# A decoder layer on one core: gates of one branch by exponential and logarithm, mLSTM in chunks of 128 tokens, and a final norm partly centred by matmuls

## The chip, the core and the metric

The kernel runs on one core of a Trainium2 chip. The metric is the device time of one launch in microseconds, the median of repeated executions. The core has a matrix engine (TensorE, PE in the profile; its weight loads are listed as PEld), three engines for elementwise work (VectorE or DVE, ScalarE or ACT, GpSimd or POOL) and a queue for transfers (SyncE, SP). Each engine works through its own instruction list in order, and semaphores make one engine wait for another.

## The reference, cut to what matters

One decoder layer is applied to a prompt of 256 tokens and to 8 single-token samples (264 columns together), everything in float32. Four token mixers run on one projection of the input and are merged by sigmoid gates; then come memory attention and an MLP with squared ReLU, each closed by a layer norm.

```python
def token_mixers(x, st, p):
    proj = x @ p["w_in"] + p["b_in"]
    ...                                   # A delta rule, B conv width 31, C short conv, D mLSTM
    out_c = bg_c * u_c
    h, C_new, n_new, m_new = mlstm_chunked(q, k, v, i_d, log_sigmoid(f_d), C_d, n_d, m_d)
    branches = jnp.stack([out_a, out_b, out_c, out_d], axis=2)
    proj_br = jnp.einsum("btnw,nwd->btnd", branches, p["w_branch"])
    gates = jax.nn.sigmoid(gate_pre.reshape(bn, T, N_BRANCH, D_MODEL))
    y = jnp.sum(gates * proj_br, axis=2) @ p["w_out"]

def step(carry, inp):                     # mLSTM, one chunk of tokens; the result doesn't depend on its length
    m_tok = jnp.maximum(b_c + m[..., None], mi_c)
    inter = jnp.exp(b_c + m[..., None] - m_tok)
    dmat = jnp.exp(ld_c - m_tok[..., None]) * qk_c
    num = inter * (q_c @ C) + dmat @ v_c
    den = inter * (q_c @ n) + sum(dmat)
    h = num / max(|den|, exp(-m_tok))
    C = scale * C + (k_c * wgt).T @ v_c

x = layer_norm(DN_ALPHA * x + sq_relu_mlp(x, p), p["ln3_g"], p["ln3_b"])
```

## The kernel before, in words

All activations stand with 128 features on the partitions and the 264 tokens in the free dimension. A large product is a list of "slots": each slot is one 128 by 1024 tile of weights (512 KB), loaded by SP into `raw`, rounded by ACT into `wh` (line 123), and the remainder `wl` = `raw` - `wh` is formed by DVE or, every few slots, by POOL (line 128). TensorE then issues 24 matmuls per slot (`mm3`, all named `g` in the profile): high by high, low by high, high by low. `feed` and `feed_lo` work two slots ahead of the matmuls.

Between slots, `run` steps generators that hold the smaller work: `chain` holds the delta rule of branch A (`a_unit`, four units of two heads) and then the mLSTM of branch D (`d_unit`, two units of two heads). A scheduler of the framework fixes the final order of each engine's list when the program is built. PSUM has two pools of four banks: `g` for the slots, `b` for everything else, handed out in turn.

Three places matter here. (1) `phase2(2, "C", True)` makes the first 16 gates and projected blocks of the merge, those of the short convolution (branch C). Its gate is `act(..., AF.Sigmoid)` straight from PSUM. The last unit of branch A and the blocks b4 to b7 of branch B run between its slots; they use the helper `sigmoid` (lines 163 to 171 hold it and `rsqrt_small`), which takes a minimum on DVE and then exponential, logarithm and exponential on ACT. `ACT_TABLE_LOAD` is the instruction that brings the tables of another function set into ACT.

(2) `d_unit` walks over four chunks of 64 tokens (`CH`). Both heads of a chunk share one PSUM bank `nb`: head 0 on partitions 0 to 63, head 1 on 64 to 127. A chunk's matmuls are `nb` from the state `C` and the queries (not in the first chunk), `nb` from the weights within the chunk (`QK`, named `m_dt`) and the values `vt`, and `cb`, the update of the state, one per head. Then a few operations on 128x1 columns (`dn`) and two passes of ACT over `nb` into `hs`, transposes `hb`, and `c_upd`, which handles four sample tokens (its matmuls are `nr`). A float32 matmul leaves two records in the trace.

(3) `tail` ends the program. `Norm.finish(True)` makes mean and 1/deviation of the last layer norm from four float32 matmuls (`s`, `q`), then `TAIL` lists eleven groups of the 16 blocks: subtract the mean, multiply by 1/deviation, apply gain and offset, send. The first of the two numbers is the count of blocks, the second says whether POOL (1) or DVE (0) does the two passes; `FIN` names two blocks whose gain and offset are on DVE, the others are on ACT.

Of the kernel before, what the change touches and what calls it, by code (L numbers as in the profile page):

```python
# [17 lines left out]
P = 128  # L18
# [11 lines left out]
NCH = NP // CH  # L30
ALPHA = 2.0 ** 0.25
# [11 lines left out]
TAIL = ((1, 0), (2, 0), (1, 1), (2, 0), (1, 1), (2, 0), (1, 1), (2, 0), (1, 1), (2, 0), (1, 0))  # L43
FIN = (11, 14)
# [40 lines left out]
for _name, _w in (("ident", 128), ("eye", 64), ("incl", 64), ("m1u", 64), ("m1t", 64), ("reset", 256)):  # L85
    _cc[_name] = (_n, _w)
    _n += _w
# [4 lines left out]
def decoder_step(ctx, tc, A, O):  # L92
# [55 lines left out]
    def mm(out, lhsT, rhs, start=True, stop=True):  # L148
        PE.matmul(out, lhsT, rhs, start=start, stop=stop)  # L149
# [234 lines left out]
    class Norm:  # L384
# [19 lines left out]
        def finish(self, last=False):  # L404
# [3 lines left out]
            for j, b in ((0, bs), (1, bq)):  # L408
                x = [a[i][:, j] if j or self.first[i] is True else self.first[i] for i in range(2)]
                if not last:  # L410
                    tt(a[0][:, j], a[0][:, j], x.pop(), ADD)
                for i, y in enumerate(x):
                    mm(b, ones, y, start=i == 0, stop=i == len(x) - 1)
            d, q = a[1][:, 0], a[1][:, 1]
            act(a[0][:, 0], bs, AF.Square, scale=n)
            act(d, bs, AF.Copy, scale=n)
# [20 lines left out]
    RD = w1.tile([P, 2, CH], F32R, name="RD")  # L437
# [6 lines left out]
    c3 = w1.tile([P, NCH, 2], F32, name="c3")  # L444
# [4 lines left out]
    GP.tensor_copy(RD[:].rearrange("p f l -> p (f l)"), zero[:].to_broadcast([P, 2 * CH]))  # L449
# [27 lines left out]
    m0, na, mp = sml[:, 0:NS], sml[:, 8:9], sml[:, 16:16 + NCH]  # L477
# [7 lines left out]
    def row_stage():  # L485
# [74 lines left out]
        cpy(d0[rD, CH:NP:CH], rb[rD, CH - 1:NP - 1:CH])  # L560
# [14 lines left out]
        for i, src in enumerate((lD, rD, lD, rD)):  # L575
            rv = RR[src, 0, 0:NP].rearrange("p (f c l) -> p f c l", f=2, c=2)
            act(RD[32 * i:32 * i + 4], rv[:, :, i // 2, :].bitcast(F32), AF.Copy)
        yield
        wg = e[rD, :]
        tt(ch(wg[:, 0:NP]), ch(LB), lastb(M, HD), SUB)  # L580
# [14 lines left out]
        for c in range(NCH):  # L595
            for hh in range(2):
                mm(b[64 * hh:64 * hh + 64, 2 * c:2 * c + 2], RR[:, 2, c * CH:(c + 1) * CH].bitcast(F32), selr[:, 8 + hh:12:2].bitcast(F32))
        cpy(c3[:].rearrange("p a b -> p (a b)"), b[:, :2 * NCH])
# [439 lines left out]
    def phase2(n, pair, first, between={}):  # L1038
        for d in range(KB):
# [3 lines left out]
            def post_g(ps, bc, d=d, st=st):  # L1043
# [3 lines left out]
                last["SIG"] = act(st["s"][:], ps, AF.Sigmoid, bias=bc)  # L1047
# [64 lines left out]
    def d_unit(u):  # L1112
# [3 lines left out]
        sh = [P, 2, 2, CH]  # L1116
        KQ = v4(bank("KQd"))
        G = bank("Gd")[:, :256].rearrange("p (h f l) -> p h f l", h=2, f=2)
# [37 lines left out]
        cpy(sl[:], ib[:, :, CH - 1:NP:CH])  # L1156
# [82 lines left out]
        for c in range(NCH):  # L1239
            hf, o = c // 2, slice(CH * (c % 2), CH * (c % 2) + CH)  # L1240
            t = slice(c * CH, c * CH + CH)
            nb = bank("nb")
            if c:
                for hh in range(2):
# [13 lines left out]
            dn = tp.tile([P, 3], F32, tag="dn", name="dn")  # L1258
            hs = w1.tile([P, 2, NP], F32, tag="wT", name="hs")
            dd, ss, rs = (dn[:, i:i + 1] for i in range(3))  # L1260
            ts(dd, nb[:, 256:257], -1.0, MUL, c3[:, c, u:u + 1], MAX)
            act(hs[:, 0], nb[:, 0:256], AF.Square, accum_out=ss)
            tt(dd, dd, nb[:, 256:257], MAX)
            recip(dd, dd)
            stt(ss, ss, dd, dd, MUL, MUL)
            rsqrt_small(rs, ss, 1.0 / 256, RMS_EPS)
            tt(rs, rs, dd, MUL)
            act(hs[:, 1], nb[:, 0:256], AF.Copy, scale=rs)
            yield
            yield from c_upd(c)  # L1270
            hb = bank("hb")[:, :256].rearrange("p (w h t) -> p w h t", w=2, h=2)
            for w in range(2):
                PE.transpose(hb[:, w].rearrange("p h t -> p (h t)"), hs[:, 1, w * P:(w + 1) * P], ident)
            for w in range(2):
                act(ho[:, :, w, t], hb[:, w], AF.Copy, scale=col("dnw", w))
# [637 lines left out]
```

## Time and profile before

| what | value |
|---|---|
| median of 3 runs | 2297.16 us (2295.27 to 2297.56) |
| the profiled execution's own time | 2294.18 us |
| its span in the trace | 2292.4 us |
| PE busy | 2239.1 us, 98% of the span |
| DVE, ACT, POOL busy | 1285.0, 1200.6, 932.1 us |
| matmul records | 19034 |

The span runs from the first to the last instruction of the program in the trace. "Busy" is the time in which an engine worked on at least one instruction; for PE it is the union of overlapping matmuls. The records of idle time name the engine whose instruction ended the wait.

### The profile page before, as it was taken

What the parts mean: (1) busy time and instruction counts of PE and PEld (TensorE: products, weight loads), DVE (VectorE), ACT (ScalarE), POOL (GpSimd) and SP (SyncE); (2) the same over time, 40 slices, a digit from 0 to 9 for tenths busy, and PEclk for the clock granted to TensorE, in tenths of its full rate; (3) what the DMA queues carried; (4) which work ended last, traced back from release to release, by engine and by line L of the source; (5) the groups of instructions that cost most, each with busy time, mean ns of one, the idle gap of its engine ahead of it and who ended that gap; (6) DMA issues with size and microseconds to landing.
All of it is one profiled execution on the core that took longest, in us unless ns stands there. A gap on an engine that the chain in (4) does not pass through costs nothing.

```text
span 2292.4 us, 46436 instructions
## 1 busy us (share of the span) xinstructions
PE 2239.1 (98%) x19034; PEld 2197.2 (96%) x19034; DVE 1285.0 (56%) x2054; ACT 1200.6 (52%) x1823; POOL 932.1 (41%) x703
## 2 busy tenths in 40 slices
PE   9899999998999999999999999999999999999997
PEld 9899999898999999999999999999999999999996
DVE  7978778576678555443465465587324324423433
ACT  6755545855566555444444454465435435534543
POOL 3523434322223123343223364136445444544576
PEclk9999999999999999999999999999999999999998
DMA  7545566454565576666566667555665566566653
GB/s 251 160 150 185 161 180 193 135 173 143 174 187 178 194 217 204 215 198 180 181 219 179 194 207 233 183 168 169 188 182 176 178 184 178 173 185 183 176 180 115
DMA packets 125134, 418.81 MB, mean 183 GB/s; under 512 B 15608, under 2 KB 20984, under 8 KB 124920
## 3 DMA queue, kind: packets, MB, share of 16 engines
q1 hardware_dynamic: 124920, 415.84, 59.1%
q8 instruction: 149, 2.44, 0.5%
q14 instruction: 65, 0.53, 0.1%
HBM read 401.37 MB, written 14.41 MB: 181 GB/s over the span
## 4 chain that ended last, share of the span: by engine, by line
PE 84%; DVE 8%; ACT 4%; issue 2%; POOL 1%; DMA 1%; SPq 0%; DVEq 0%; ACTq 0%; POOLq 0%
PE g L149 74%; PE q L149 3%; DVE wl L128 2%; ACT L123 1%; DVE cB L138 1%; DVE cu L138 1%; PE pv L149 1%; ACT wh L123 1%; DVE s L138 1%; DVE y L128 1%; DMA dbc<-dd 1%; PE xb L149 0%; PE ob L149 0%; PE ub L149 0%; ACT sg L123 0%
## 5 line engine op out<-in xcount | busy, mean ns | idle before, releaser
L123 ACT ACTIVATE wh<-raw 128x1024 fp32r<-128x1024 f32 (+1 forms) x705 | 744.0, 1057 | 766.7 <-PE g L149 594.3
L128 POOL TENSOR_TENSOR wl<-raw,wh 128x1024 fp32r<-128x1024 f32 x234 | 571.3, 2441 | 652.8 <-PE g L149 466.5
L149 PE MATMUL g<-xh,wl 128*128 128x264 f32 x2496 | 712.2, 285 | 6.7 <-DVE wl L128 6.6
L128 DVE TENSOR_TENSOR wl<-raw,wh 128x1024 fp32r<-128x1024 f32 (+1 forms) x471 | 591.5, 1256 | 226.2 <-PE g L149 129.2
L149 PE MATMUL g<-xh,wh 128*128 128x264 f32 x2496 | 717.1, 287 | 0.0
L149 PE MATMUL g<-xl,wh 128*128 128x264 f32 x2496 | 714.0, 286 | 0.0
L149 PEld LDWEIGHTS g<-xh,wl 128*128 128x128 f32 x2496 | 471.2, 189 | 9.4 <-DVE wl L128 8.0
L149 PEld LDWEIGHTS g<-xh,wh 128*128 128x128 f32 x2496 | 471.9, 189 | 5.8 <-issue 3.4
L149 PEld LDWEIGHTS g<-xl,wh 128*128 128x128 f32 x2496 | 470.5, 189 | 1.2 <-issue 0.8
L149 PE MATMUL g<-hgh,wl 128*128 128x264 f32 x1024 | 290.4, 284 | 0.0
L149 PE MATMUL g<-hgl,wh 128*128 128x264 f32 x1024 | 290.4, 284 | 0.0
L149 PE MATMUL g<-hgh,wh 128*128 128x264 f32 x1024 | 289.9, 284 | 0.0
L149 PE MATMUL g<-zh,wh 128*128 128x266 f32 x960 | 275.0, 286 | 0.0
L149 PE MATMUL g<-zh,wl 128*128 128x266 f32 x960 | 274.9, 286 | 0.1
L149 PE MATMUL g<-zl,wh 128*128 128x266 f32 x960 | 274.6, 286 | 0.0
L149 PEld LDWEIGHTS g<-hgl,wh 128*128 128x128 f32 x1024 | 193.0, 188 | 0.0
L149 PEld LDWEIGHTS g<-hgh,wh 128*128 128x128 f32 x1024 | 192.6, 188 | 0.0
L149 PEld LDWEIGHTS g<-hgh,wl 128*128 128x128 f32 x1024 | 192.3, 188 | 0.0
L149 PEld LDWEIGHTS g<-zl,wh 128*128 128x128 f32 x960 | 181.7, 189 | 0.0
L149 PEld LDWEIGHTS g<-zh,wl 128*128 128x128 f32 x960 | 180.8, 188 | 0.8 <-POOL wl L128 0.8
L149 PEld LDWEIGHTS g<-zh,wh 128*128 128x128 f32 x960 | 181.4, 189 | 0.0
L128 DVE TENSOR_TENSOR hgl<-relu,hgh 128x264 fp32r<-128x264 f32 x64 | 60.7, 950 | 173.7 <-ACT hgh L123 173.7
(482 smaller groups left out, 3436.8 us busy)
## 6 DMA issues: line engine op xcount, KB each, us to landing
raw<-in_win_dram SPq DMA_DIRECT2D x312, 512.0 KB, 4.0
raw<-in_f_dram SPq DMA_DIRECT2D x248, 512.0 KB, 4.0
raw<-in_wbr_dram SPq DMA_DIRECT2D x64, 512.0 KB, 4.3
raw<-in_wout_dram SPq DMA_DIRECT2D x32, 512.0 KB, 4.2
s<-in_sS_dram SPq DMA_DIRECT2D x8, 512.0 KB, 5.3
dbc<-dd SPq DMA_DIRECT2D x16, 256.0 KB, 4.1
out_S_s_dram<-s SPq DMA_DIRECT2D x8, 512.0 KB, 5.3
c<-in_sCm_dram SPq DMA_DIRECT2D x8, 512.0 KB, 5.4
```

Source lines behind the costliest of these rows:

```text
L123: return AC.activation(out, in_, func, bias=bias, scale=scale, **kw)
L128: return (eng or DV).tensor_tensor(out=out, in0=a, in1=b, op=op)
L138: return DV.scalar_tensor_tensor(out=out, in0=a, scalar=s, in1=b, op0=op0, op1=op1)
L149: PE.matmul(out, lhsT, rhs, start=start, stop=stop)
```

## The change

It has three parts.

First, `phase2` with `n == 2` calls `sigmoid(st["s"], ps, bc)`: a DVE operation that adds the bias and bounds from below, then Exp, Ln and Exp on ACT. The other three phases keep `AF.Sigmoid`.

Second, `d_unit` walks over two chunks of 128 tokens (`CD`). The decay matrix `E` and the weights `QK` are now 128 by 128 per head and chunk; `QK` lies in `UB`, a tile that branch A no longer needs then. Each head gets its own bank `nb` with all 128 partitions as tokens. `row_stage` makes the scans and columns for chunks of 128 (the 16 small matmul records of `emT` become four, and the four copies into `RD` go).

Third, in `tail` the negative mean is kept; blocks 10 to 15 are centred on PE (identity times block, plus identity times negative mean, both float32, into six PSUM banks), and DVE alone does the passes: "s" adds the negative mean to two blocks, "m" multiplies two blocks by 1/deviation, "p" multiplies one block from PSUM. All gains and offsets are on ACT; POOL does nothing in it.

```diff
-TAIL = ((1, 0), (2, 0), (1, 1), (2, 0), (1, 1), (2, 0), (1, 1), (2, 0), (1, 1), (2, 0), (1, 0))
-FIN = (11, 14)
+PE_TAIL = 10
+TAIL = (("s", 0, 2), ("s", 2, 2), ("m", 0, 2), ("p", 10, 1), ("s", 4, 2), ("m", 2, 2), ("p", 11, 1), ("m", 4, 2),
+        ("s", 6, 2), ("p", 12, 1), ("m", 6, 2), ("s", 8, 2), ("p", 13, 1), ("m", 8, 2), ("p", 14, 1), ("p", 15, 1))
...
-            act(d, bs, AF.Copy, scale=n)
+            act(d, bs, AF.Copy, scale=-n if last else n)
...
-                last["SIG"] = act(st["s"][:], ps, AF.Sigmoid, bias=bc)
+                if n == 2:
+                    sigmoid(st["s"][:], ps, bc)
+                else:
+                    last["SIG"] = act(st["s"][:], ps, AF.Sigmoid, bias=bc)
...
-            mm(G[:, hh], selc(h0 + hh), RD[:])
-        for hf, hh, o, t in each():
-            mm(KQ[o, hf, hh], k[:, hh, t], q[:, hh, t])
-        E, QK = mat("m_dl"), mat("m_dt")
+            mm(G[:, hh], sel(8 + h0 + hh, P), RR[:, 0, 0:NP])
+        for hf in range(2):
+            for hh in range(2):
+                t = slice(hf * P, hf * P + P)
+                mm(KQ[:, hf, hh], k[:, hh, t], q[:, hh, t])
+        QK = UB
...
-        for c in range(NCH):
-            hf, o = c // 2, slice(CH * (c % 2), CH * (c % 2) + CH)
-            t = slice(c * CH, c * CH + CH)
-            nb = bank("nb")
-            if c:
-                for hh in range(2):
-                    mm(nb[64 * hh:64 * hh + 64, :257], qi[:, hh, t], C[:, hh, :], stop=False)
+        for c in range(NCD):
+            t = slice(c * CD, c * CD + CD)
+            nbs = [bank("nb") for hh in range(2)]
             for hh in range(2):
-                mm(nb[64 * hh:64 * hh + 64, :257], QK[o, hf, hh], vt[o, hf, hh, :], start=c == 0)
+                if c:
+                    mm(nbs[hh][:, :257], qi[:, hh, t], C[:, hh, :], stop=False)
+                mm(nbs[hh][:, :257], QK[:, c, hh], vt[:, c, hh, :], start=c == 0)
...
-                mm(cbs[hh], kw[o, hf, hh], vt[o, hf, hh])
+                mm(cbs[hh], kw[:, c, hh], vt[:, c, hh])
...
+        for d in range(PE_TAIL, KB):
+            ps = (gbank if d < PE_TAIL + 4 else bank)("ctr")[:, :NT]
+            last["PE"] = after(mm(ps, ident, y3[:, d, :], start=True, stop=False), "PE")
+            mm(ps, ident, ln.mu, start=False, stop=True)
+            centred[d] = ps
+        def step_(i, n, kind):
+            t = y3[:, i:i + n, :]
+            if kind == "s":
+                x = tt(t, t, ln.mu[:, None, :].to_broadcast([P, n, NT]), ADD)
+            elif kind == "m":
+                x = tt(t, t, ln.rs[:, None, :].to_broadcast([P, n, NT]), MUL)
+            else:
+                x = tt(y3[:, i, :], centred[i], ln.rs, MUL)
+            last["T"] = after(x, "T")
+            if kind == "s":
+                return
+            for j in range(i, i + n):
+                act(y3[:, j, :], y3[:, j, :], AF.Identity, bias=col("l3b", j), scale=col("l3g", j))
+            SP.dma_start(O["y"][:, i:i + n, :], t)
```

How the order of instructions moves at three places. ACT while the last unit of branch A normalises its queries and keys (`rq`, `rk`) and a block of branch B makes its gate (`gB`), between the slots of `phase2(2)`; before:

```order
L123 ACT_TABLE_LOAD
L123 ACTIVATE gB<-gB 128x264
L123 ACT_TABLE_LOAD
L123 ACTIVATE rk<-ssk,eps 128x2x256
L123 ACT_TABLE_LOAD
L123 ACTIVATE rq<-rq 128x528
L123 ACT_TABLE_LOAD
L123 ACTIVATE gB<-gB,ones 128x264
L123 ACTIVATE wh<-raw 128x1024
L123 ACT_TABLE_LOAD
L123 ACTIVATE gB<-gB 128x264
L123 ACT_TABLE_LOAD
```

and now, with `gate` the gate of branch C:

```order
L127 ACTIVATE gB<-gB 128x264
L127 ACTIVATE rk<-ssk,eps 128x2x256
L127 ACTIVATE rq<-rq 128x528
L127 ACTIVATE gB<-gB,ones 128x264
L127 ACTIVATE wh<-raw 128x1024
L127 ACTIVATE gB<-gB 128x264
L127 ACTIVATE rk<-ss_6597,eps 128x2x8
L127 ACTIVATE rk<-rk 128x528
L127 ACTIVATE cB<-extB,pc 128x256
L127 ACTIVATE wh<-raw 128x1024
L127 ACTIVATE gate<-gate 128x264
L127 ACTIVATE gate<-gate,ones 128x264
```

The loads are gone, and each `gate` has three operations. In the whole list of ACT there are 50 loads before and 7 now.

TensorE at a chunk of the first mLSTM unit that has a state (`hs` the normalised output, `vtD` the values, `kwD` the weighted keys); before, one of three such chunks of 64 tokens:

```order
L149 MATMUL g<-xh,wl 128x264
L1273 MATMUL hb<-cst,hs 128x128 x2
L149 MATMUL nb<-C,qkvD 64x257 x2
L149 MATMUL nb<-vtD,m_dt 64x257 x2
L149 MATMUL cb<-vtD,kwD 128x257 x2
L149 MATMUL g<-xh,wh 128x264
```

and now, the only one, of 128 tokens:

```order
L153 MATMUL g<-xh,wl 128x264
L153 MATMUL nb<-C,qkvD 128x257
L153 MATMUL nb<-vtD,UB 128x257
L153 MATMUL nb<-C,qkvD 128x257
L153 MATMUL nb<-vtD,UB 128x257
L153 MATMUL cb<-vtD,kwD 128x257 x2
L153 MATMUL g<-xh,wh 128x264
```

The shapes are output partitions by columns: the two 64-partition halves of `nb` have become two full matmuls, and the chunk occurs once instead of three times. The first `nr` afterwards follows 24 `g` later in both.

The tail on DVE (`a` holds mean and 1/deviation, 128x528 is two blocks), before:

```order
L138 SCALAR_TENSOR_TENSOR a_26062<-q,a_26061 128x264
L128 TENSOR_TENSOR y<-y,a_26062 128x264
L128 TENSOR_TENSOR y<-y,a_26062 128x528
L128 TENSOR_TENSOR y<-y,a_26062 128x264
L128 TENSOR_TENSOR y<-y,a_26062 128x528 x8
L128 TENSOR_TENSOR y<-y,a_26062 128x264
L128 TENSOR_TENSOR y<-y,a_26062 128x528
L134 TENSOR_SCALAR y<-y,pc 128x264
L128 TENSOR_TENSOR y<-y,a_26062 128x264
L134 TENSOR_SCALAR y<-y,pc 128x264
```

and now:

```order
L142 SCALAR_TENSOR_TENSOR a_26028<-q,a_26027 128x264
L132 TENSOR_TENSOR y<-y,a_26028 128x528 x3
L132 TENSOR_TENSOR y<-ctr,a_26028 128x264
L132 TENSOR_TENSOR y<-y,a_26028 128x528 x2
L132 TENSOR_TENSOR y<-ctr,a_26028 128x264
L132 TENSOR_TENSOR y<-y,a_26028 128x528 x2
L132 TENSOR_TENSOR y<-ctr,a_26028 128x264
L132 TENSOR_TENSOR y<-y,a_26028 128x528 x2
L132 TENSOR_TENSOR y<-ctr,a_26028 128x264
L132 TENSOR_TENSOR y<-y,a_26028 128x528
L132 TENSOR_TENSOR y<-ctr,a_26028 128x264 x2
```

with TensorE's last rows now

```order
L153 MATMUL s<-a_26027,ones 128x264
L153 MATMUL q<-a_26027,ones 128x264
L153 MATMUL s<-y,ones 128x264
L153 MATMUL q<-a_26028,ones 128x264
L153 MATMUL ctr<-y,cst 128x264 x6
L153 MATMUL ctr<-a_26028,cst 128x264 x6
```

DVE has taken over what POOL did, and TensorE issues all six products with the blocks before the six with the mean.

## Rows read from the trace of the kernel before

**Rows 1.** The page of the profile: busy time, share and instructions of PE, and the clock granted to it in 40 slices of the span (9 is 90% or more of full speed).

```profile
PE 2239.1 (98%) x19034; PEld 2197.2 (96%) x19034; DVE 1285.0 (56%) x2054; ACT 1200.6 (52%) x1823; POOL 932.1 (41%) x703
...
PEclk9999999999999999999999999999999999999998
```

**Rows 2.** Busy time by stretch: limits and length of the stretch in us, then busy us (and instructions) of each engine, PE's granted clock, the share of the transfer engines and GB/s.

```profile
50.00:100.00 50.00, 44.16 (x352) 42.61 (x351) 46.12 (x82) 36.98 (x72) 32.30 (x40) 0.93 0.46 141
100.00:375.00 275.00, 269.97 (x2561) 262.90 (x2560) 215.09 (x381) 148.32 (x264) 109.37 (x129) 1.00 0.57 174
400.00:655.00 255.00, 234.43 (x2175) 228.35 (x2174) 168.33 (x301) 171.45 (x252) 74.30 (x80) 0.98 0.52 158
757.00:972.00 215.00, 215.00 (x1752) 200.44 (x1751) 110.39 (x227) 111.27 (x187) 65.17 (x43) 1.00 0.68 210
524.70:528.80 4.10, 4.08 (x26) 3.75 (x27) 3.52 (x9) 4.05 (x5) 0.93 (x2) 0.50 0.45 132
```

**Rows 3.** Waits of PE between 400 and 655 us: waiting operation, the instruction it waited for, us in total, times, the longest.

```profile
PE KQ L149 <- DVE qkv L128: 9.0, 1, 9.0
PE ob L149 <- ACT dl L123: 3.5, 3, 2.1
...
PE ss L149 <- ACT rq L123: 2.3, 1, 2.3
```

**Rows 4.** The timeline of PE between 515 and 529 us: start, duration of the row, operation, count.

```profile
515.36 0.40 PE L149 MATMUL G<-RA,selw 128*128 128x256 f32 x2
524.72 1.98 PE L149 MATMUL KQ<-qkv 128*64 128x128 f32 x16 [8.96 <-DVE qkv L128]
```

**Rows 5.** The timeline of ACT between 507 and 524 us; between the first and the last row of table loads shown there are eight, both counted.

```profile
507.61 1.28 ACT L123 ACT_TABLE_LOAD   x1
...
521.58 1.28 ACT L123 ACT_TABLE_LOAD   x1
522.87 0.64 ACT L123 ACTIVATE rk<-rk 128x528 f32<-128x528 f32 x1
```

**Rows 6.** Groups of ACT's instructions between 375 and 655 us: count, busy us, mean ns of one, idle time before them.

```profile
L123 ACT ACT_TABLE_LOAD x41 | 52.6, 1283 | 0.7
L123 ACT ACTIVATE gate<-g,pc 128x264 f32<-128x264 f32 x15 | 7.1, 472 | 0.1
L123 ACT ACTIVATE sg<-sg 128x264 f32<-128x264 f32 x12 | 5.1, 423 | 3.9 <-DVE sg L133 3.8
...
L123 ACT ACTIVATE sg<-sg,ones 128x264 f32<-128x264 f32 x6 | 3.1, 517 | 0.1
```

**Rows 7.** A group of DVE's instructions over the whole span: the first operation of the helper `sigmoid` from PSUM, in branch B.

```profile
L134 DVE TENSOR_SCALAR gB<-g,pc 128x264 f32<-128x264 f32 x8 | 3.9, 489 | 9.3 <-PE g L149 9.1 <-POOL qkv L128 0.2
```

**Rows 8.** The timeline of PE around a chunk of the first mLSTM unit.

```profile
796.19 0.29 PE L149 MATMUL g<-xh,wl 128*128 128x264 f32 x1
796.31 0.38 PE L1273 MATMUL hb<-cst,hs 128*128 128x128 f32 x2
796.62 0.65 PE L149 MATMUL nb<-C,qkvD 128*64 128x257 f32 x4
797.21 0.65 PE L149 MATMUL nb<-vtD,m_dt 64*64 64x257 f32 x4
797.79 1.13 PE L149 MATMUL cb<-vtD,kwD 64*128 64x257 f32 x4
...
799.08 0.28 PE L149 MATMUL g<-xl,wh 128*128 128x264 f32 x1
```

**Rows 9.** The timeline of PE around float32 matmuls with all 128 rows and columns (memory attention).

```profile
1480.61 0.28 PE L149 MATMUL pv<-wh,meml 128*128 128x256 f32 x1
1480.73 1.46 PE L149 MATMUL av<-att 128*128 128x256 f32 x6
...
1482.14 0.28 PE L149 MATMUL pv<-wh,memh 128*128 128x256 f32 x1
```

**Rows 10.** The timeline of PE at the start of the first mLSTM unit.

```profile
757.95 0.28 PE L149 MATMUL g<-xh,wl 128*128 128x264 f32 x1
...
758.33 0.69 PE L149 MATMUL KQd<-qkvD 128*64 128x64 f32 x16
...
759.18 0.28 PE L149 MATMUL g<-xl,wh 128*128 128x264 f32 x1
```

**Rows 11.** The timeline of ACT after the chunk of rows 8: the last reader of the bank `nb`.

```profile
800.85 0.48 ACT L123 ACTIVATE hs<-nb,dn 128x256 f32<-128x256 f32 x1 [2.21 <-DVE dn L128]
```

**Rows 12.** Groups of DVE's instructions by shape, first between 2279 and 2284 us, then between 2286.3 and 2287.8 us.

```profile
L128 DVE TENSOR_TENSOR y<-y,a 128x528 f32<-128x528 f32 x5 | 5.9, 1242 | 0.0
...
L128 DVE TENSOR_TENSOR y<-y,a 128x528 f32<-128x528 f32 x2 | 1.4, 697 | 0.0
L128 DVE TENSOR_TENSOR y<-y,a 128x264 f32<-128x264 f32 x1 | 0.4, 420 | 0.0
```

**Rows 13.** The last row of ACT's timeline, in the tail.

```profile
2285.70 3.48 ACT L123 ACTIVATE y<-y,pc 128x264 f32<-128x264 f32 x6 [0.73 <-DVE y L128]
```

**Rows 14.** The timeline of PE at its end, of DVE and of POOL in the tail, one row of each.

```profile
2275.13 0.61 PE L149 MATMUL q<-a,ones 128*128 128x264 f32 x2
...
2276.20 11.67 DVE L128 TENSOR_TENSOR y<-y,a 128x264 f32<-128x264 f32 x13
...
2277.43 7.67 POOL L128 TENSOR_TENSOR y<-y,a 128x264 f32<-128x264 f32 x7 [0.55 <-ACT a L123]
```

More of the change, by code (lines that the diff above doesn't have):

```diff
@@ L30 @@
 NCH = NP // CH
+CD = 128
+NCD = NP // CD
 ALPHA = 2.0 ** 0.25
@@ L84 @@
 _n = 0
[L85 removed]
+for _name, _w in (("ident", 128), ("eye", 64), ("incl", 64), ("incd", 128), ("m1u", 64), ("m1t", 64), ("reset", 256)):
     _cc[_name] = (_n, _w)
@@ L148, in mm @@
     def mm(out, lhsT, rhs, start=True, stop=True):
-        PE.matmul(out, lhsT, rhs, start=start, stop=stop)
+        return PE.matmul(out, lhsT, rhs, start=start, stop=stop)
     MUL, ADD, SUB, MAX, MIN = ALU.mult, ALU.add, ALU.subtract, ALU.max, ALU.min
@@ L412, in finish @@
                 for i, y in enumerate(x):
-                    mm(b, ones, y, start=i == 0, stop=i == len(x) - 1)
+                    last_mm = mm(b, ones, y, start=i == 0, stop=i == len(x) - 1)
+            marks["stats"] = last_mm
             d, q = a[1][:, 0], a[1][:, 1]
             act(a[0][:, 0], bs, AF.Square, scale=n)
-            act(d, bs, AF.Copy, scale=n)
+            act(d, bs, AF.Copy, scale=-n if last else n)
             stt(q, bq, n, a[0][:, 0], MUL, SUB)
@@ L443, in decoder_step @@
     c2 = w1.tile([P, 2, 4, 8], F32, name="c2")
-    c3 = w1.tile([P, NCH, 2], F32, name="c3")
+    c3 = w1.tile([P, NCD, HD], F32, name="c3")
     rowt = X16("rowt", F32)
@@ L1257, in d_unit @@
             C = Cn
-            dn = tp.tile([P, 3], F32, tag="dn", name="dn")
             hs = w1.tile([P, 2, NP], F32, tag="wT", name="hs")
[L1260 to L1268, printed above, removed]
-            yield
[L1270 to L1275, printed above, removed]
+            for hh in range(2):
+                nb = nbs[hh]
+                dn = tp.tile([P, 3], F32, tag="dn", name="dn")
+                dd, ss, rs = (dn[:, i:i + 1] for i in range(3))
+                ts(dd, nb[:, 256:257], -1.0, MUL, c3[:, c, h0 + hh:h0 + hh + 1], MAX)
+                act(hs[:, hh], nb[:, 0:256], AF.Square, accum_out=ss)
+                tt(dd, dd, nb[:, 256:257], MAX)
+                recip(dd, dd)
+                stt(ss, ss, dd, dd, MUL, MUL)
+                rsqrt_small(rs, ss, 1.0 / 256, RMS_EPS)
+                tt(rs, rs, dd, MUL)
+                act(hs[:, hh], nb[:, 0:256], AF.Copy, scale=rs)
+            yield
+            for hh in range(2):
+                yield from c_upd(2 * c + hh)
+                if hh == 0:
+                    hb = bank("hb")[:].rearrange("p (h w t) -> p h w t", h=2, w=2)
+                    for h in range(2):
+                        for w in range(2):
+                            PE.transpose(hb[:, h, w], hs[:, h, w * P:(w + 1) * P], ident)
+                    for w in range(2):
+                        act(ho[:, :, w, t], hb[:, :, w], AF.Copy, scale=col("dnw", w))
         store(O["C_p"][:, h0:h0 + 2, :], C[:, :, 0:256])
@@ L1745, in tail @@
             pass
[L1746 to L1772 removed]
+        centred = {}
+        last["PE"] = marks["stats"]
+        for d in range(PE_TAIL, KB):
[17 more added lines that the diff above has]
+            SP.dma_start(O["y"][:, i:i + n, :], t)
+        for kind, i, n in TAIL:
+            step_(i, n, kind)
     mark(tail)
```

79 lines of the change are left out of this document (26 added, 53 removed).

## The prediction

> **What bounds the kernel now.** I read the page first: TensorE is busy for 2239.1 us, 98% of the span, at full clock in nearly every slice [rows 1]. So the time is TensorE's work plus about 53 us in which it stands still, and a change pays only if it shortens TensorE's own list, removes a stall of it, or shortens the stretch before its first and after its last instruction. The second view, busy time by stretch, says where the stalls are [rows 2]: 50 to 100 us (5.8 us idle, the start), 100 to 375 (5.0), 400 to 655 (20.6, the stretch of `phase2(2)`), and none from 757 to 972, the mLSTM. There every matmul less is time less. The third view, the waits of 400 to 655, shows one dominant stall: `KQ`, 9.0 us [rows 3], on TensorE's timeline between 515 and 525 us [rows 4]. It is put down to a product on DVE, but what came late in front of that is on ACT: from 507.61 us on, eight table loads stand before the last exponential of `rk` at 522.87 [rows 5], 8 x 1.28 = 10.3 us of 15.3. After the stall TensorE runs at half clock, 0.50 for 4.1 us [rows 2], which costs 4.1 x 0.5 = 2.05 us.
>
> **Part 1, the gates.** Of 50 table loads 43 go. In the stretch there are 41, of 1283 ns each, with only 0.7 us idle in front of all of them together [rows 6]. ACT thus gets back 43 x 1.283 = 55.2 us and pays, per gate, two exponentials (0.423 each) and a logarithm (0.517) for the sigmoid (0.472) [rows 6]: 0.891 x 16 = 14.3. Net 41 us. DVE gets 16 operations of 0.489 [rows 7], 7.8 us more, at 168 busy of 255 [rows 2].
>
> None of that is TensorE's, so what counts is how much of its 20.6 us of stall was caused by the loads. `KQ` was, and the waits `ob` and `ss` name ACT too (3.5 and 2.3) [rows 3]; the rest are `wl`, `ub` and `db`, smaller ones. As a measure of what remains I take 100 to 375 us: the same units of branch A between slots, no switching of tables, 5.03 us idle of 275 [rows 2], which is 5.03 x 255 / 275 = 4.7 us for 255. Gain: 20.6 - 4.7, and with 2.05 of half clock **18 us**. Lower bound: only `KQ` and its half clock go (11.05) and all new DVE time appears on the path (7.8): 3 us. Upper bound: every stall goes, 20.6 + 2.05 = 22.6. I take 18, near the upper end, since the row it rests on is the same work without loads, and since TensorE has work two slots ahead, 2 x 24 x 0.121 = 5.8 us (0.121 is a `g` matmul's step: 796.31 - 796.19 and 1480.73 - 1480.61 [rows 8, 9]); a DVE operation of 0.5 us per slot fits under that.
>
> **Part 2, the mLSTM.** Before, one chunk with a state: from the `g` at 796.19 to the next after it at 799.08, 2.89 us, less two `g` [rows 8], so 2.65 for `hb`, both `nb` and `cb`. The first chunk lacks the `nb` from the state (797.21 - 796.62 = 0.59) and the preceding `hb` (0.22): 1.84. With a last `hb` and the start of the unit, `Gd` and `KQd`, 1.23 less two `g` = 0.99 [rows 10], a unit is 3 x 2.65 + 1.84 + 0.22 + 0.99 = 11.0 us.
>
> After, all matmuls are 128 by 128. A float32 record of that shape and 256 columns is shown in memory attention: 1.53 us from `g`-like to `g`-like matmul, less two steps, over six records, 0.215 us [rows 9]. The first chunk has 8 records (two `nb`, two `cb`, two records each), 1.73; the second 12, 2.59; `hb` is unchanged, 4 x 0.22 = 0.87; `G` 0.24 and `KQ` 0.87 (records of half the columns at half the time). Sum 6.3. Saved per unit 4.7, in two units **9.4 us**. TensorE never idles here [rows 2], so it is one to one unless a wait is new.
>
> A rule speaks against this saving. The old chunk's rows are 0.58 us for each pair of `nb` and 799.08 - 797.79 less one `g`, 1.17 us, for the pair of `cb` [rows 8]. The Trainium skill, "TensorEngine Tiling (Array Packing)", Theoretical Speedup, promises up to twice the speed where one dimension is at most 64, by tiles that run side by side. By that rule each old pair would be two records' time, 0.43, the old unit 0.87 + 11 x 0.43 + 0.99 = 6.6 us, and the change would save next to nothing, 0.6 us in two units, the time some 2275. The trace disagrees, with 0.58 and 1.17 where the rule has 0.43, so the measurement decides and I give the rule no chance beyond what lies in the lower bound of 4 and the range; that the same page's Key Properties has a change of the tiling mode drain the engine would fit the difference.
>
> The new wait could be PSUM: `nb`, `nb`, `cb`, `cb` take all four `b` banks, and the next `nr` needs the first again. Before, the last `hs` that reads `nb` ended at 801.33 [rows 11], 3.5 us after the last `nb` matmul issued (797.8 [rows 8]). After, the first head's last `nb` comes 1.73 us before the end of `cb` and the second's 0.87; with the same 3.5 us their banks come free 1.8 and 2.7 us after `cb`, and `nr` follows 24 `g` after it, 2.9 us. So it just fits; if it doesn't, the price is up to 1 us in each of four chunks. Bounds 4 to 10.
>
> **Part 3, the tail.** Before, ACT ends at 2285.70 + 3.48 = 2289.2 [rows 13] and the transfers 3.2 us later. DVE takes 1.24 us for two blocks while POOL works beside it and 0.70 when POOL is quiet [rows 12]. After, POOL is silent: DVE has ten operations of 0.70 and six of one block, 0.42: 9.5 us from 2276.20 [rows 14]. TensorE has its last sum at 2275.13 [rows 14]; from its end at 2275.6, twelve records of 0.22 and the first of the products with the mean (0.44) put block 10 at 2278.7. DVE would want it after three operations, at 2278.3, so about 0.7 us of waits, end 2286.4. ACT then has one more block, 0.6, at 2287.0; its own 16 blocks at 3.48 / 6 = 0.58 [rows 13] from 2277.9 end at 2287.2. Against 2289.2 I take **2.2 us**. If TensorE is at half clock there, its products come 1.5 to 3 us later: 0.7. If the DVE passes overlap as closely as 11.67 us for 13 mixed ones could under a quiet POOL, 3.5.
>
> Not counted: the small `emT` records (12 fewer, 0.4 us) and a changed order of DVE and ACT during start-up.
>
> **The sum.** 18 + 9.4 + 2.2 = 29.6 us. Against the profiled execution's own 2294.18 that is 2264.6. The median of the runs is 3.0 higher, 2297.16, and so 2267.6. I say 2266, between the two.
>
> **Rivals.**
> (A) The stall changes hands. `KQ` waits for DVE [rows 3], DVE gets 7.8 us more work there, and `wl` is made by DVE: with term 1 worth 5 to 10 instead of 18, the time is 2297 - (17 to 22), 2275 to 2280. For it: the releaser named is DVE. Against it: 168 us of 255 busy, and 10.3 us of loads sit before the chain that DVE waited for. Chance 0.14.
> (B) More goes than the stretch: ACT, ahead by 41 us, also takes down the stalls at either end of it, or the reordered start loses its 5.8 us idle and the next stretch part of its 5.0 [rows 2]: with what I left of term 1, 10 to 15 us more, 2251 to 2256. Chance 0.08.
> (C) Slower, by one mechanism: DVE works in order. Each new gate's first operation waits for TensorE's accumulation, the product of the gate with the projected block waits behind it for three operations on ACT, each behind a `wh` in ACT's list, and the next `wl` stands behind both. Then TensorE waits for `wl` once per gate. From 29.6 / 16 = 1.85 us per gate on it eats the whole gain; at 2.2 it makes 2303. For it: the three operations are 1.36 us, and a `wh` between them adds some more. Against it: the same helper is used eight times by branch B [rows 7] and by branch A's units between 100 and 375 us with 5 us of idle in all [rows 2], and two slots are in hand. Chance 0.03.
> (D) The change doesn't do what it says: if exponential and logarithm each bring a load, 16 x 3 x 1.283 = 62 us more on ACT stand in place of 55 removed; the stall stays and only 9.4 + 2.2 are left, 2285. The order of instructions now shows no load between them. Chance 0.02. On this the Trainium skill, "ScalarE: Activation LUTs", What ACT_TABLE_LOAD costs, puts a switch at 1283 ns and a further 1380 ns of drain. The trace agrees on the first; 0.7 us idle ahead of 41 loads shows nothing of the second. By that rule ACT would get back 43 x 2.66 = 114 us, which leaves the bound on term 1, every stall, as it is.
>
> **How the numbers follow.** The forecast has 0.73, with its own range 2257 to 2274 (term 1 from 13 to 21, term 2 from 6 to 10, term 3 from 0.7 to 3.5, and some 3 us between executions). To hold the time 8 times in 10 I take in most of A and part of B: 2254 to 2279. About 0.2%, 4.6 us, is what a measurement of this kernel can tell from no change. Faster by more than that: forecast, A, B and D, less the few of A and D in which the terms fall near their lower bounds (3 + 4 + 0.7 = 7.7 is still faster): 0.95. Slower 0.03, from C, and 0.02 within.
>
> **What would show it.** Part 1: no loads between 400 and 655 us, `KQ` waits under 1 us, TensorE idle there near 5 us and no half clock after it; if the idle stays above 12 and names DVE or `wl`, A is right. Part 2: no idle in the mLSTM, `nb` records of about 0.215 us per step, a unit 4.7 us shorter; a wait of `nr` for `hs` would show the banks short. Part 3: DVE operations of 0.70 throughout, first `ctr` from the mean near 2.6 us after the last `q`, and 2 us less between the last sum and the end. My forecast is wrong if TensorE's idle time moves to the stretches around `phase2(2)` in place of vanishing, or if its records in the mLSTM don't become shorter than the trace of memory attention says.

## The result, and the profile after

The changed kernel takes 2262.7 us (median of 4 runs, 2261.86 to 2263.22) against 2296.36 us for the kernel before (4 runs, 2295.27 to 2297.56) timed beside it: a ratio of 0.9853 with a 95% interval of 0.9836 to 0.9870. The prediction, 2266, lies 3.3 us above it. The profiled execution took 2262.53 us with a span of 2260.7, so between the two profiled executions the span fell by 31.7 us.

The page of the changed kernel, PE's busy time and its clock by slices; these answer to [rows 1]:

```profile
PE 2231.2 (99%) x18982; PEld 2198.5 (97%) x18982; DVE 1285.3 (57%) x2062; ACT 1157.4 (51%) x1802; POOL 923.1 (41%) x694
...
PEclk9999999999999999999999999999999999999999
```

TensorE's busy time fell by 7.9 us; the other 23.8 us of the span were time in which it stood still. Most of that shows in busy time by stretch (columns as in [rows 2]; the mLSTM now lies at 737 to 945):

```profile
50.00:100.00 50.00, 43.89 (x340) 42.59 (x340) 46.34 (x82) 36.08 (x68) 31.13 (x41) 0.93 0.47 141
100.00:375.00 275.00, 270.88 (x2569) 263.81 (x2568) 215.00 (x382) 149.37 (x266) 109.22 (x128) 1.00 0.58 174
400.00:655.00 255.00, 251.05 (x2337) 246.10 (x2337) 194.61 (x336) 142.58 (x250) 80.35 (x78) 1.00 0.58 175
737.00:945.00 208.00, 208.00 (x1705) 202.19 (x1704) 107.46 (x222) 110.19 (x180) 69.76 (x45) 1.00 0.71 221
```

The start and the stretch up to 375 us are nearly as they were (6.1 and 4.1 us idle, 5.8 and 5.0 before). In 400 to 655 the idle time is 3.95 us instead of 20.57, the clock 1.00 instead of 0.98, and in the mLSTM there is no idle time, as before. Some 7.5 us less of standing still are in the tail, but 5.5 of them only because TensorE now works on `ctr` there. The waits of PE in 400 to 655, against [rows 3]:

```profile
PE g L153 <- DVE wl L132: 1.7, 2, 1.3
PE xb L153 <- DVE m_u L132: 1.4, 1, 1.4
PE ss L153 <- ACT rq L127: 0.8, 1, 0.8
```

`KQ` and `ob` no longer wait at all. Because stretches shift, I compare the two traces at the same piece of work: the moment when ACT has finished rounding the weights (`wh`) of the slot with the same number.

| slot (of 705) | before, us | after, us | difference | what lies since the row above |
|---|---|---|---|---|
| 108 | 385.7 | 385.2 | -0.6 | start and phase 1 |
| 204 | 736.0 | 715.6 | -20.3 | the gates of branch C: 19.7 gained |
| 288 | 1016.1 | 986.6 | -29.5 | mLSTM: 9.2 gained |
| 696 | 2240.0 | 2210.5 | -29.5 | nothing |
| end of span | 2292.4 | 2260.7 | -31.7 | tail: 2.2 gained |

The prediction had 18, 9.4 and 2.2 for the three parts. A chunk of the mLSTM with a state is now, on PE's timeline (the one of [rows 8] was 64 tokens, this one is 128):

```profile
792.07 0.28 PE L153 MATMUL g<-xh,wl 128*128 128x264 f32 x1
792.19 0.60 PE L153 MATMUL nb<-C,qkvD 128*128 128x257 f32 x2
792.62 0.60 PE L153 MATMUL nb<-vtD,UB 128*128 128x257 f32 x2
793.06 0.59 PE L153 MATMUL nb<-C,qkvD 128*128 128x257 f32 x2
793.49 0.60 PE L153 MATMUL nb<-vtD,UB 128*128 128x257 f32 x2
793.93 1.03 PE L153 MATMUL cb<-vtD,kwD 128*128 128x257 f32 x4
...
794.92 0.28 PE L153 MATMUL g<-xl,wh 128*128 128x264 f32 x1
```

Twelve records in 794.92 - 792.07 less two steps of 0.121 = 2.61 us, 0.217 each. The tail, DVE's groups by shape between 2246 and 2258 us, then the last row of ACT's timeline, then PE's last three, then two rows of DVE's timeline (two passes of two blocks, and its last passes):

```profile
L132 DVE TENSOR_TENSOR y<-y,a 128x528 f32<-128x528 f32 x10 | 6.6, 701 | 0.0
L132 DVE TENSOR_TENSOR y<-ctr,a 128x264 f32<-128x264 f32 x6 | 2.5, 429 | 0.8 <-PE ctr L153 0.8
```

```profile
2251.07 6.61 ACT L127 ACTIVATE y<-y,pc 128x264 f32<-128x264 f32 x13 [0.62 <-DVE y L132]
```

```profile
2245.61 0.61 PE L153 MATMUL q<-a,ones 128*128 128x264 f32 x2
2246.06 2.83 PE L153 MATMUL ctr<-y,cst 128*128 128x264 f32 x12
2248.73 2.83 PE L153 MATMUL ctr<-a,cst 128*128 128x264 f32 x12
```

```profile
2252.87 1.32 DVE L132 TENSOR_TENSOR y<-y,a 128x528 f32<-128x528 f32 x2
2255.07 0.77 DVE L132 TENSOR_TENSOR y<-ctr,a 128x264 f32<-128x264 f32 x2
```

Against [rows 12 to 14]: the two-block pass is 0.70 us throughout, DVE waits 0.8 us once for the first product with the mean, and from the last `q` to the end of the span it is 15.1 us, where it was 2292.4 - 2275.13 = 17.3.

The sum was right, so the runs ask whether the reasons were: what in part 1 removes the loads and why they cost what they cost, what part 2's gain consists of, and which half of part 3 pays.

### The profile page after: what moved, and what is told of

It is laid out like the page before. It is cut to its first block, busy times and chain, and to the rows that moved or that the text cites. A ratio compares the mean times of both kernels' runs of the same rounds, so it can differ in the third digit from the quotient of the medians.

```text
span 2260.7 us, 46321 instructions
## 1 busy us (share of the span) xinstructions
PE 2231.2 (99%) x18982; PEld 2198.5 (97%) x18982; DVE 1285.3 (57%) x2062; ACT 1157.4 (51%) x1802; POOL 923.1 (41%) x694
## 4 chain that ended last, share of the span: by engine, by line
PE 88%; DVE 8%; ACT 2%; POOL 1%; issue 1%; DMA 1%; SPq 0%; ACTq 0%; DVEq 0%; POOLq 0%
PE g L153 78%; PE q L153 3%; DVE wl L132 2%; DVE cB L142 1%; PE pv L153 1%; DVE cu L142 1%; DVE s L142 1%; DMA dbc<-dd 1%; PE xb L153 1%; PE ub L153 1%; PE ob L153 0%; ACT wh L127 0%; PE db L153 0%; PE sb L153 0%; PE tb L153 0%
```

## Experiments on the gates

**Part 1 alone.** The kernel before with the new gate of branch C and nothing else:

```diff
-                last["SIG"] = act(st["s"][:], ps, AF.Sigmoid, bias=bc)
+                if n == 2:
+                    sigmoid(st["s"][:], ps, bc)
+                else:
+                    last["SIG"] = act(st["s"][:], ps, AF.Sigmoid, bias=bc)
```

> The kernel before with part 1 alone: the 16 gates by exponential and logarithm, 7 table loads instead of 50, mLSTM and tail as before. My theory, that the parts are independent: the stretches of the two traces give part 1 19.7 us, so 2296.4 - 19.7 = 2276.7 us (2274 to 2279). Rival, that part of the gain seen in that stretch came by way of the other parts (free banks, another order): 2282 or more.

Measured: 2275.2 us (2274.11 to 2276.47) against 2295.9 beside it, ratio 0.9905 (0.9890 to 0.9920). The difference, 20.7 us, is that of the stretch (19.7) within what such runs scatter: part 1 stands by itself. The stretch, columns as above:

```profile
400.00:655.00 255.00, 251.17 (x2338) 246.22 (x2337) 194.91 (x337) 142.26 (x250) 80.23 (x78) 1.00 0.57 175
```

**One gate by Sigmoid again.** The reason for this run stands in ACT's timeline of the kernel before, behind the first row of [rows 5]:

```profile
509.78 1.28 ACT L123 ACT_TABLE_LOAD   x1
511.07 0.43 ACT L123 ACTIVATE gB<-gB 128x264 f32<-128x264 f32 x1
511.51 1.28 ACT L123 ACT_TABLE_LOAD   x1
512.81 0.69 ACT L123 ACTIVATE rk<-ssk,eps 128x512 f32<-128x512 f32 x1
513.52 1.28 ACT L123 ACT_TABLE_LOAD   x1
```

None of these loads stands at a gate of branch C. They stand between the exponentials (`gB`) and the logarithms (`rk<-ssk,eps`) of branches A and B. The program loads one set with both functions at its start, and between 100 and 375 us no load occurs; the first Sigmoid removes that set, and from there on exponential and logarithm fetch a set each time they alternate. If that is so, a single Sigmoid is enough. The edit to the changed kernel:

```diff
-                if n == 2:
+                if n == 2 and d != 0:
                     sigmoid(st["s"][:], ps, bc)
```

> The changed kernel with one of the 16 gates, the first, by AF.Sigmoid again. The built list of ACT then has 71 table loads instead of 7, nearly all between exponential and logarithm of branches A, B and the other 15 gates. My theory (the loads come from losing the one set that holds both functions, wherever it is lost, and they cost where they stand in a chain that TensorE waits for): 64 x 1.283 = 82 us more on ACT, TensorE idle between 400 and 655 us at 20 us or more again, 2282 to 2305 us. Rival, as my prediction counted it (the sum of 43 loads goes with the 16 gates, 2.7 loads per gate): one sixteenth of 19.7, 1.2 us, 2264 us.

Measured: 2294.3 us (2292.1 to 2297.27), ratio to before 0.9992 (0.9982 to 1.0001). One gate of 16 costs 31.6 us, about as much as all three parts gained together. But parts 2 and 3 kept their gain here: the whole loss lies between slots 108 and 204, which take 362.2 us where the changed kernel takes 330.5 and the kernel before 350.2. So a single Sigmoid, with 15 gates of the new form behind it, makes this stretch slower than 16 Sigmoids did. The loads between 375 and 655 us, the stretch, then the two longest waits of PE in it:

```profile
L127 ACT ACT_TABLE_LOAD x55 | 70.6, 1283 | 1.0
```

```profile
400.00:655.00 255.00, 230.34 (x2094) 224.04 (x2094) 173.88 (x304) 190.46 (x277) 70.52 (x73) 0.96 0.49 149
```

```profile
PE KQ L153 <- DVE qkv L132: 8.9, 1, 8.9
PE g L153 <- DVE wl L132: 5.9, 2, 3.7
```

The wait of `KQ` is back at its old length, and the granted clock falls to 0.96, below the 0.98 of the kernel before. ACT's timeline says why it is worse than before: of the 41 loads of [rows 6] only 7 stood directly ahead of a gate of branch C. Here one stands ahead of the Sigmoid, 30 are again outside these gates, and 24 are within the new gates, whose exponentials and logarithms alternate too.

**The same gate, with the set restored**, in the changed kernel:

```diff
-                if n == 2:
+                if n == 2 and d != 0:
                     sigmoid(st["s"][:], ps, bc)
                 else:
                     last["SIG"] = act(st["s"][:], ps, AF.Sigmoid, bias=bc)
+                    if n == 2:
+                        after(AC.preload_act_table_set("natural_log_exp_and_others"), "SIG")
```

> As the run before, the first gate by AF.Sigmoid, but the set that holds exponential and logarithm is loaded again right behind it: 9 table loads in all. My theory: 2262 to 2264 us, no difference from the changed kernel. Rival (the form of the first gate itself, Sigmoid on ACT in place of DVE and three operations, costs the time): the same as the run before, over 2275.

Measured: 2261.6 us (2260.59 to 2261.78), ratio 0.9845 (0.9830 to 0.9859). That is just below the 2262 to 2264 expected. There are two loads between 375 and 655 us instead of 55, and one more load, placed by hand, is worth 32.7 us. So it was neither the form of that gate nor its order, but the set it left behind.

```profile
L127 ACT ACT_TABLE_LOAD x1 | 1.3, 1283 | 0.0
L1051 ACT ACT_TABLE_LOAD x1 | 1.3, 1283 | 0.0
```

**All 16 gates by Sigmoid, the set restored behind each**, in the kernel before, mLSTM and tail untouched:

```diff
                 last["SIG"] = act(st["s"][:], ps, AF.Sigmoid, bias=bc)
+                if n == 2:
+                    pre = AC.preload_act_table_set("natural_log_exp_and_others")
+                    after(pre, "SIG")
```

> The kernel before with all 16 gates still by AF.Sigmoid, but the set that holds exponential and logarithm loaded again behind each: 39 table loads instead of 50, none of them between an exponential and a logarithm; 32 stand around the gates. Theory place (a load costs where it stands in a chain that TensorE waits for, not by its sum): close to the kernel with part 1 alone, 2276 to 2280 us. Theory amount (each load costs its share of the 19.7 us, 0.46): 11 of 43 are gone, 2296.4 - 5 = 2291 us.

Measured: 2273.3 us (2272.4 to 2273.71), ratio 0.9895 (0.9879 to 0.9912), below even the kernel with part 1 alone and 2.7 us below the range of theory place; theory amount, 2291 us, is out. The stretch, and the loads between 375 and 655 us:

```profile
400.00:655.00 255.00, 252.84 (x2354) 248.09 (x2353) 189.03 (x327) 170.46 (x252) 82.75 (x81) 1.00 0.58 175
```

```profile
L123 ACT ACT_TABLE_LOAD x16 | 20.5, 1283 | 0.3
L1049 ACT ACT_TABLE_LOAD x16 | 20.5, 1283 | 0.3
```

This is the run that tells amount from place. ACT is busy for 170.5 us of the stretch, as in the kernel before (171.5 [rows 2]), and TensorE's idle time is 2.2 us instead of 20.6. 41 us of loads around the gates cost nothing that can be seen: the two waits of PE that are left there, 1.3 us for `wl` and 0.8 for `rq`, name no gate. In the kernel before, 10.3 us of loads in the chain of `rk` went with a wait of 9. The Trainium skill, "ScalarE: Activation LUTs", Table sets: the hidden batching unit, says that one set holds both exponential and logarithm, so that the two need one load; the traces agree as long as nothing else is called (no load between 100 and 375 us). After one Sigmoid the two did not share a set again until it was asked for.

**More DVE in each gate**, for rivals A and C of the prediction. In the changed kernel:

```diff
                 if n == 2:
+                    for _ in range(4):
+                        ts(st["s"][:], ps, bc, ADD, -80.0, MAX)
                     sigmoid(st["s"][:], ps, bc)
```

> The changed kernel with the first DVE operation of each of the 16 gates five times instead of once (the result is the same): 64 x 0.489 = 31 us more of DVE in the stretch of the gates. Tests rival C of the prediction, a DVE that works in order and makes `wl` late. Theory (two slots in hand cover it): at most 5 us more, 2262 to 2268 us. Rival (each gate's DVE time comes out on TensorE): 31 us more, 2294 us.

Measured: 2264.7 us (2262.91 to 2265.17), 2.0 above the changed kernel for 31 us of DVE, too little to tell by the times alone. The stretch and its longest wait:

```profile
400.00:655.00 255.00, 250.03 (x2327) 245.00 (x2326) 218.68 (x395) 140.88 (x250) 82.60 (x78) 1.00 0.56 173
```

```profile
PE g L153 <- DVE wl L132: 3.7, 3, 1.6
```

Of 24 us more DVE in this stretch 1.0 us reaches TensorE. `wl` is late three times for 3.7 us, where the changed kernel has two times and 1.7, and not at 16 gates: some of rival C's queue is there, and what TensorE has in hand covers nearly all of it.

## Experiments on the mLSTM

**The pairs issued twice**, in the kernel before:

```diff
             for hh in range(2):
-                mm(nb[64 * hh:64 * hh + 64, :257], QK[o, hf, hh], vt[o, hf, hh, :], start=c == 0)
+                mm(nb[64 * hh:64 * hh + 64, :257], QK[o, hf, hh], vt[o, hf, hh, :], start=c == 0, stop=False)
+            for hh in range(2):
+                mm(nb[64 * hh:64 * hh + 64, :257], QK[o, hf, hh], vt[o, hf, hh, :], start=False)
...
-                mm(cbs[hh], kw[o, hf, hh], vt[o, hf, hh])
+                mm(cbs[hh], kw[o, hf, hh], vt[o, hf, hh], stop=False)
+                mm(cbs[hh], kw[o, hf, hh], vt[o, hf, hh], start=False)
```

> The kernel before with the pair `nb` from `QK` and `vt` and the pair `cb` each issued twice in every chunk of 64 tokens (accumulated, so those values are doubled). Read from TensorE's timeline: a chunk with a state costs 2.65 us now. Theory one (records of 64-wide tiles run two side by side in `nb`, 7 ns apart, and one after the other in `cb` at 0.22, and the rest of the 2.65 is paid once at each change of the tile's form): the second pairs add 0.43 to 0.52 and 0.87, 3.95 to 4.05 us. Theory two (as my prediction read it: every such pair costs 0.58 and 1.17, whatever stands before it): 4.4 us.

Measured, one execution: 2305.4 us against 2295.2 beside it. PE's timeline of the first chunk with a state, to be set against [rows 8]:

```profile
798.20 0.28 PE L149 MATMUL g<-xh,wl 128*128 128x264 f32 x1
798.33 0.38 PE L1276 MATMUL hb<-cst,hs 128*128 128x128 f32 x2
798.64 0.65 PE L149 MATMUL nb<-C,qkvD 128*64 128x257 f32 x4
799.22 1.08 PE L149 MATMUL nb<-vtD,m_dt 64*64 64x257 f32 x8
800.24 2.00 PE L149 MATMUL cb<-vtD,kwD 64*128 64x257 f32 x8
...
802.39 0.28 PE L149 MATMUL g<-xl,wh 128*128 128x264 f32 x1
```

From `nb<-vtD` to `cb` it is 1.02 us for eight records where it was 0.58 for four: the second pair adds 0.44. From `cb` to the second `g` behind it is 2.15 against 1.29: the second four add 0.86. The chunk, 802.39 - 798.20 less two steps, is 3.95 us: theory one. The second `nb` pair, four records, took the time of two: the heads' 64-column tiles did run side by side. The `cb` matmuls, which share the same 64 rows, took 0.215 each, as full tiles do. Eight chunks with 1.30 us more each make 10.4, the whole difference of this run (10.2). What then makes the first 0.58 and 1.17 us longer?

**The same matmuls in another order**, in the kernel before:

```diff
             if c:
                 for hh in range(2):
                     mm(nb[64 * hh:64 * hh + 64, :257], qi[:, hh, t], C[:, hh, :], stop=False)
+            mm(cbs[0], kw[o, hf, 0], vt[o, hf, 0])
             for hh in range(2):
                 mm(nb[64 * hh:64 * hh + 64, :257], QK[o, hf, hh], vt[o, hf, hh, :], start=c == 0)
-            for hh in range(2):
-                mm(cbs[hh], kw[o, hf, hh], vt[o, hf, hh])
+            mm(cbs[1], kw[o, hf, 1], vt[o, hf, 1])
```

(The declarations of `Cn` and `cbs` move up, and the order is pinned with `after`.)

> The kernel before with the same matmuls of each chunk in another order: `nb` from the state, `cb` of head 0, `nb` from `QK`, `cb` of head 1, one change of the tile's form more per chunk. Theory one (a change costs about 0.1 us, from the 0.32 of the first `cb` record against 0.22 of the next): 2.72 to 2.85 us per chunk with a state. Theory two (the price belongs to the record's shape, not to the order): 2.65 us.

Measured, one execution: 2298.5 us against 2295.2 beside it, of which the mLSTM's chunks explain 8 x 0.19 = 1.5 us. The rest lies ahead of the mLSTM, at the gates, where this execution has the granted clock at 0.50 in two more short stretches, at 435 and 653 us, than the profile of the kernel before. The chunk:

```profile
799.14 0.29 PE L149 MATMUL g<-xh,wl 128*128 128x264 f32 x1
799.27 0.38 PE L1273 MATMUL hb<-cst,hs 128*128 128x128 f32 x2
...
802.22 0.28 PE L149 MATMUL g<-xl,wh 128*128 128x264 f32 x1
```

802.22 - 799.14 less two steps is 2.84 us against 2.65: one more change of the tile's form costs 0.19, about twice the 0.1 of theory one, though the chunk lies just within its range. So the old chunk divides into 0.22 for `hb`, eight record times of 0.217 (two for each `nb` pair, four for `cb`; only the pair from `QK` was doubled, and the pair from the state is taken to be like it), 1.74, and what is left, 0.69, for four changes of form, 0.17 each on average. That the price lies in the form and not in a new bank or new operands shows in the changed kernel: its groups are all 128*128, they follow each other in 0.43 or 0.44 us for two records, and nothing is added between them. Per unit the change saves eight `cb` records (1.74), two record times of `nb` (14 to 12, 0.43), and the changes of form of four chunks (3 x 0.69 + 0.54 = 2.61); the start costs 0.13 more (0.99 to 1.12). That makes 4.65; the old and new groups of the two units, summed, differ by 9.1, 4.56 per unit. By this estimate more than half of part 2 is the changes of form.

The Trainium skill, "TensorEngine Tiling (Array Packing)", states both halves: Theoretical Speedup, that tiles of 64 run at up to twice the rate, which the added `nb` pair shows (0.44 us for what one after the other would take 0.87), and Key Properties, that a change of the tiling mode drains the engine, which the other order prices at 0.19 us here.

## Experiments on the tail

**No centring on TensorE**, all passes on DVE, POOL idle as in the changed kernel:

```diff
-PE_TAIL = 10
-TAIL = (("s", 0, 2), ("s", 2, 2), ("m", 0, 2), ("p", 10, 1), ("s", 4, 2), ("m", 2, 2), ("p", 11, 1), ("m", 4, 2),
-        ("s", 6, 2), ("p", 12, 1), ("m", 6, 2), ("s", 8, 2), ("p", 13, 1), ("m", 8, 2), ("p", 14, 1), ("p", 15, 1))
+PE_TAIL = 16
+TAIL = (("s", 0, 2), ("s", 2, 2), ("m", 0, 2), ("s", 4, 2), ("m", 2, 2), ("s", 6, 2), ("m", 4, 2), ("s", 8, 2),
+        ("m", 6, 2), ("s", 10, 2), ("m", 8, 2), ("s", 12, 2), ("m", 10, 2), ("s", 14, 2), ("m", 12, 2), ("m", 14, 1), ("m", 15, 1))
```

> The changed kernel without the centring on TensorE: all 16 blocks get both passes on DVE, POOL still does nothing there. From the last `g` to the end of the span the kernel before has 18.5 us and the changed one 16.4. Theory one (the gain of part 3 is POOL's silence, which brings DVE's two-block pass from 1.24 to 0.70 us): DVE needs 15 x 0.62 + 0.7 after 2246.7, 0.9 us later than the changed kernel, and ACT, whose queue of 0.51 us per block sets the end, is hardly later: 16.4 (16.1 to 17.2) us, time within 1 us of 2262.7. Theory two (the centring on TensorE brings it): 18 us or more, 2264.5 and above.

Measured: 2262.7 us (2262.24 to 2264.7), ratio 0.9852 (0.9838 to 0.9867); no difference from the changed kernel can be told by the times. By the trace the last `q` starts at 2244.82 and the span ends at 2260.5: 15.7 us, against 15.1 with the centring and 17.3 before.

```profile
2244.82 0.61 PE L152 MATMUL q<-a,ones 128*128 128x264 f32 x2
```

```profile
2247.86 9.53 ACT L126 ACTIVATE y<-y,pc 128x264 f32<-128x264 f32 x16 [0.88 <-DVE y L131]
```

So the passes on DVE alone, with POOL silent, bring 1.6 us of the 2.2, and the products on TensorE 0.5 to 0.6. The run doesn't part POOL's silence from the new grouping of the passes, nor from the two gains and offsets that moved to ACT; the next run takes up the last of these. (The figures 18.5 and 16.4 in the expectations are the stretch from the last `g`; read exactly it is 18.7 and 16.6, and 17.1 in this run.)

**Two gains and offsets on DVE**, in the changed kernel, as the kernel before had:

```diff
+FIN = (12, 15)
...
-                act(y3[:, j, :], y3[:, j, :], AF.Identity, bias=col("l3b", j), scale=col("l3g", j))
+                if j in FIN:
+                    last["T"] = after(ts(y3[:, j, :], y3[:, j, :], col("l3g", j), MUL, col("l3b", j), ADD), "T")
+                else:
+                    act(y3[:, j, :], y3[:, j, :], AF.Identity, bias=col("l3b", j), scale=col("l3g", j))
```

> The changed kernel with gain and offset of blocks 12 and 15 on DVE instead of ACT. Theory (in the changed tail ACT sets the end: its last 13 operations follow each other without idle time, 0.51 each, and end 1.8 us after DVE): two of them less, DVE 0.7 us longer, the end 0.5 to 1.1 us earlier, about 15.6 us from the last `g` to the end. Rival (DVE or the last transfers set the end): 16.4 us or 0.3 to 0.7 more.

Measured: 2262.8 us (2260.51 to 2263.67), ratio 0.9849 (0.9835 to 0.9864), and by the trace 15.3 us from the last `q` at 2246.10 to the end at 2261.4, 0.2 more than without the edit. My theory fell. ACT does end earlier, 13.1 us after the last `g` instead of 13.5, but the end does not follow. The three last sends on SP's queue:

```profile
2257.26 1.30 SPq L1780 DMA_DIRECT2D out_y_dram<-y  x3
```

They go out one behind the other, three in 1.30 us, the last one 13.5 us after the last `g`, just where the changed kernel has it (2257.71 - 2244.16). With ACT and DVE both a little ahead, the sends of single blocks at the end of SP's list are what the profile shows last.

## Put together

The restored sets in the changed kernel, with and without the last edit, and the changed kernel itself once more.

> The changed kernel with two edits that the runs point to: the 16 gates by AF.Sigmoid again with the set of exponential and logarithm loaded behind each (32 loads around the gates, no DVE operation), and gain and offset of two tail blocks on DVE. Theory: the run with all sets restored was 1.9 us below the one with part 1 alone, the tail gives 0.5 to 1: 2260 us (2258.5 to 2262). Rival (32 loads on ACT delay the mLSTM's or the gates' chains here): 2263 or more.

> The changed kernel once more, unaltered, as the yardstick for the next run on the same chip: 2261 to 2264 us.

> The changed kernel with all 16 gates by AF.Sigmoid and the set of exponential and logarithm restored behind each; its tail unaltered. If the restored sets are worth anything over the other form of the gate, as the two runs without the new mLSTM and tail suggest (2273.3 against 2275.2), it is 1 to 2 us below the run beside it; if the difference was scatter of single builds, within 1 us of it. Its stretch of the gates alone should gain about 1 us, by the idle time of TensorE there (2.2 against 3.9 us).

Measured: with both edits 2260.7 us (2260.14 to 2263.2), ratio 0.9844 (0.9829 to 0.9859), against 2260.45 with the restored sets alone (below): the tail edit adds nothing that can be seen here either. The changed kernel again 2262.2 (2261.63 to 2263.33), ratio 0.9851 (0.9837 to 0.9864), and beside it the one with restored sets 2260.45 (2259.74 to 2262.16), ratio 0.9845 (0.9831 to 0.9858). The intervals overlap, so by the times it is not settled that this beats the changed kernel. The stretch of the gates can place about 1 us of the 1.8: 2.4 us idle against 255 - 251.63 = 3.4 in the run beside it (the pair with the old mLSTM and tail has 2.2 against 3.8):

```profile
400.00:655.00 255.00, 252.60 (x2334) 248.00 (x2331) 188.50 (x325) 170.32 (x252) 82.02 (x78) 1.00 0.59 176
```

## Why the prediction was right, and where it was not

**Term 1, 18 us; measured 19.7.** The size came from the step "as a measure of what remains I take 100 to 375 us": it left 4.7 us of idle time, 3.95 remain, and the half clock is gone as said. Idle time is 16.6 us of the 19.7; of the other 3.1, in TensorE's busy time, the half clock is 2.05 by the prediction's reckoning, and 1 us stays open. Rivals A and C are out: `KQ` waits for nothing now, and four more DVE operations per gate cost 1.0 us in the stretch, not 24. B is out, as the idle time on either side hardly moved, and D, as no load is left between 375 and 655 us. What the working did not ask is why 43 loads go; rival D priced loads by the gate ("16 x 3 x 1.283"). With one Sigmoid 30 loads stand outside the gates of branch C, where the kernel before has 34, and the gates need not change form at all: a restored set gives 20 us or more with Sigmoid kept.

**Term 2, 9.4 us; measured 9.2.** Right in the sum, since it took durations from rows at both ends, and the banks fitted: no wait appeared. Wrong in one reading: "the trace disagrees, with 0.58 and 1.17 where the rule has 0.43". The pairs of `nb` did run side by side; their 0.58 held two record times and a change of form, which the two added pairs and the other order took apart. For `cb` there was nothing to pack. Had I forecast a variant of the old chunk from "0.58 per pair" instead of this change, I would have been off, 4.4 us where 3.95 was measured.

**Term 3, 2.2 us; measured 2.2.** Most steps held: 0.70 per pass, one wait of 0.8 for the first `ctr` (0.7 predicted), no half clock while TensorE works. Two sizes missed and met in the right number, which is luck. DVE ended 10.2 us after the start of the last `q`, not 11.3, since passes overlap (1.32 us for two of 0.70). "ACT then has one more block, 0.6" was 1.8: ACT's last 13 operations follow each other without a break and set the end, 12.1 us after that `q`, where the prediction's other reckoning, 16 blocks of 0.58, also had it (2287.2 - 2275.13). And ACT is not alone: the last sends on SP set the end as well, as the two blocks moved to DVE showed.

**The sum.** 31.7 us between the profiled executions against 29.6 predicted; the median of the changed kernel lies on its profiled execution (2262.53), not 3 us above it as for the kernel before. These two make up the 3.3 us.

## What to carry to other kernels

Read what stands before and behind each table load: if it separates functions that one set holds, look for the one call that threw the set out, and either replace that call or load the set again right behind it, in a place with cover. Count a load by the chain it stands in, not by the sum. When matmuls of unlike tile forms alternate, price the changes as well as the records: double a group to get the price of a record, and reorder it to get that of a change.

## What the runs showed of the hardware that was not expected

One Sigmoid among 16 gates raised the number of table loads from 7 to 71 and took 31.6 us; one load behind it took the time back and left 9 loads. ACT busy for the same 170 us in the same stretch went with 20.6 or 2.2 us of idle time on TensorE. Two 64-column tiles ran two records in one record's time (0.22 us), and a change between tile forms cost 0.17 to 0.19 us.
